# Hybrid decoder block: norm weights spread by a product with ones, the meta tokens' norm and the bias table later, idle transposes at the start

## The chip, the cores and the metric

The kernel runs on one core of a Trainium2 chip. TensorE (PE) multiplies matrices, VectorE (DVE), ScalarE (ACT) and GpSimd (POOL) work elementwise, and SyncE (SP) issues all DMA. Each engine works off its own instructions in a fixed order and waits for others on semaphores. Operands lie in SBUF; TensorE writes to PSUM, which has eight banks of 128 partitions by 512 fp32 values. The metric is device time in microseconds, the median over runs.

## What is computed

One decoder block over 1040 tokens (16 meta tokens, then 1024 tokens of input) of width 1024. Only the beginning matters here: the first norm, and the projection of its result.

```python
def rms_norm(x, g, eps=1e-6):
    xf = x.astype(jnp.float32)
    y = xf * lax.rsqrt(jnp.mean(xf * xf, axis=-1, keepdims=True) + eps)
    return (y * g.astype(jnp.float32)).astype(x.dtype)
...
    h = jnp.concatenate([meta, x], axis=1)
...
        u = rms_norm(h, norm_mix[l])
        proj = u @ w_in[l]
        qa, ka, va, qf, kf, vf, fl, xc, yc, gates = jnp.split(proj, split_points, axis=-1)
```

After that come a sliding-window attention with a bias by distance (`rel_bias_table`), a forgetting attention, a recurrence with a short convolution (fed by `xc`, `yc`), gates, an output projection and a SwiGLU layer, with residuals and a final norm. The inputs and the output are fp32.

## The kernel before

**Products.** Every fp32 operand of a large product is split in two fp32r parts, a high part (a rounded copy by ScalarE, L118 or L138) and a low part (what is left, by VectorE at L119 or GpSimd at L139). A product is three passes: high by high, high by low, low by high (`mm3`, L151).

**The start.** Tokens come in tiles: tile 0 is the 16 meta tokens, tiles 1 to 8 are 128 tokens each. `load_x` (L284) loads a tile to one of four `xt` buffers. `normed` (L293) has ScalarE square it and sum (L298, into one of three `xg` buffers), take the root (L299), VectorE take the reciprocal (L300) and, in two halves of 512 columns, multiply by it and by the norm weights `gbc` (L302). `gbc` holds the weights on all 128 partitions; one DMA broadcasts them there from DRAM (512 KB written). `to_feature_major` (L199) then transposes the tile on TensorE (L205, eight pieces of 128 columns, four to a bank) and splits it into `uh` and `ul`, in which features lie on partitions and tokens along the row.

**The first projection.** The block's products begin with two slices of the weights for `xc` (`x0h`, `x0l`, `x1h`, `x1l`), in chunks of tokens: chunk `FULL[0]` is tokens 0 to 271, that is tiles 0, 1 and 2, and its products read all three. 24 products with 272 columns make a chunk (eight pieces of the features, three passes each). Tiles 3 and 4 follow (`FULL[1]`), then the slices for `yc` and tiles 5 to 8.

**The bias table.** `pb` is a product of the 32-row table with one-hot rows (L322, plain fp32), to which a mask row is added (L323). It is written to DRAM and read back on all partitions some 20 us later, and used in the attention.

**What sets the order.** A scheduler of the tile framework orders each engine's instructions when the kernel is built; `keep_in_program_order` and `issue_after` bind it. The order is fixed from then on. Behind the first 45 us of work it is the same in both kernels.

Of the kernel before, what the change touches and what calls it, by code (L numbers as in the profile page):

```python
# [46 lines left out]
def f32(ap):  # L47
    return ap.bitcast(F32)
# [3 lines left out]
def hybrid_block(ctx, tc, h_in, w_in, w_v0, w_v1, w_bd, par, rows, gains, relt, onehot,  # L52
# [4 lines left out]
    def dma(dst, src):  # L57
        nc.sync.dma_start(f32(dst) if dst.dtype == F32R else dst, f32(src) if src.dtype == F32R else src)
# [20 lines left out]
    def nm(s):  # L79
        uid[0] += 1  # L80
        return f"{s}_{uid[0]}"
# [73 lines left out]
    def run(gen):  # L155
        for _ in gen:
            pass
# [38 lines left out]
    def halves(x):  # L196
        return x[:, :512], x[:, 512:]

    def to_feature_major(xg, n, uh, ul, off):  # L199

        for half in range(2):
            pt = tr_bank()
            for i in range(4):
                k = 4 * half + i
                pe.transpose(pt[:, i * P:i * P + n], xg[:n, k * P:(k + 1) * P], ident[:n, :n])  # L205
            src = pt.rearrange("p (i q) -> p i q", i=4)[:, :, :n]
            ks = slice(4 * half, 4 * half + 4)
            split(uh[:, ks, off:off + n], ul[:, ks, off:off + n], src)

    def u_tile(c, a):  # L210
        if c:
# [64 lines left out]
    ra = ctx1.enter_context(tc.tile_pool(name="ra", bufs=1, side="right", reuse_waits="tile"))  # L276
    pad(ra, 128)
    with tc.tile_pool(name="r0", bufs=1, side="right", reuse_waits="tile") as r0:
        gbc = r0.tile([P, D], F32, name="gbc")

        def rows_of(t):
            return (NM, 0) if t == 0 else (P, NM + (t - 1) * P)

        def load_x(t):  # L284
            n, t0 = rows_of(t)
            xt = r0.tile([P, D], F32, tag="xt", bufs=4, name=nm("xt"))
            dma(xt[:n], h_in[t0:t0 + n])
            return xt

        def norm_in(t, xt):  # L290
            to_feature_major(*normed(t, xt))

        def normed(t, xt):  # L293
            n, t0 = rows_of(t)
            c, off = (0, t0) if t0 < W0 else (1, t0 - W0)
            xg = r0.tile([P, D], F32, tag="xg", bufs=3, name=nm("xg"))
            q = cp.tile([P, 1], F32, tag="sq", bufs=4, name=nm("sq"))
            act.activation(xg[:n], xt[:n], AF.Square, accum_out=q[:n])  # L298
            act.activation(q[:n], q[:n], AF.Sqrt, bias=epst[:n], scale=1.0 / D)  # L299
            dve.reciprocal(q[:n], q[:n])  # L300
            for x, y, z in zip(*(halves(v[:n]) for v in (xg, xt, gbc))):
                dve.scalar_tensor_tensor(x, y, q[:n], z, ALU.mult, ALU.mult)  # L302
            return xg, n, uh[c], ul[c], off

        xts = [load_x(t) for t in range(2)]
        dma(gbc, gains[0:1].partition_broadcast(P))
        xts.append(load_x(2))
        n0, n1 = normed(0, xts[0]), normed(1, xts[1])
        to_feature_major(*n1)
        n2 = normed(2, xts[2])  # L310
        to_feature_major(*n0)
        to_feature_major(*n2)

        dma(cmt, cmask)
        rt = r0.tile([32, 8], F32, name="rt")
        oh = r0.tile([32, 383], F32, name="oh")
        mr = r0.tile([8, 383], F32, name="mr")
        dma(rt, relt)
        dma(oh, onehot)
        dma(mr, maskrow.partition_broadcast(8))  # L320
        pb = sc_bank()
        pe.matmul(pb[:8, :383], rt, oh, start=True, stop=True)  # L322
        dve.tensor_tensor(mr, pb[:8, :383], mr, ALU.add)  # L323
        sinks = [x_sinks(ra, m) for m in range(2)]
        wx = [load_w(w_in[XC + m], D, r0, f"x{m}", lo_on_pool=True) for m in range(2)]
        xs34 = [load_x(t) for t in (3, 4)]
        n34 = [normed(t, xs34[t - 3]) for t in (3, 4)]
        for m in range(2):
            run(proj_chunk(XC + m, wx[m], FULL[0], sinks[m][0]))
            if m == 0:  # L330
                to_feature_major(*n34[0])
                to_feature_major(*n34[1])
        for m in range(2):
            run(proj_chunk(XC + m, wx[m], FULL[1], sinks[m][0]))
        xs56 = [load_x(t) for t in (5, 6)]
        wy = [load_w(w_in[YC + m], D, lo_on_pool=True) for m in range(2)]
        for t in range(5, 7):
            norm_in(t, xs56[t - 5])
        run(proj_chunk(YC, wy[0], REAL[0], sinks[0][1]))
        for t in range(7, 9):  # L340
            norm_in(t, load_x(t))
        dma(part, par)
        dma(rowt, rows.partition_broadcast(P))
        dve.tensor_scalar(nsink, rowt[:, 0:8], -1.0, None, ALU.mult)
        dma(bts, mr)
        pad(r0, 32)
        bb = r0.tile([P, 8, 383], F32, name="bb")
        dma(bb, bts.partition_broadcast(P))
        dma(bss, bb)
        run(proj_chunk(YC + 1, wy[1], REAL[0], sinks[1][1]))  # L350
        for m in range(2):
            run(proj_chunk(XC + m, wx[m], FULL[2], sinks[m][0]))
        for m in range(2):
            run(proj_chunk(YC + m, wy[m], REAL[1], sinks[m][1]))
# [928 lines left out]
```

## Time and profile before

| what | value |
|---|---|
| median of 3 runs | 1650.19 us (1649.83 to 1652.05) |
| the profiled execution | 1652.01 us, span 1650.2 us |
| TensorE busy | 1627.5 us, 99% of the span |
| VectorE, ScalarE, GpSimd busy | 1006.8, 759.7, 389.4 us |
| TensorE's first instruction | 9.28 us |
| first product of the first projection | 15.51 us |

The span runs from the first to the last instruction; the time of a run has 1.8 us more around it. TensorE's busy share is near the whole span, so what counts is when its stream begins and what waits inside it.

### The profile page before, as it was taken

To read this page: it belongs to the slowest core of one execution; us is meant where nothing else is said; L and a number is where in the kernel's file an instruction comes from. 1 tells how busy PE (TensorE), PEld (TensorE's weight loads), DVE (VectorE), ACT (ScalarE), POOL (GpSimd) and SP (SyncE) were. 2 spreads that over 40 slices of the span, in tenths; PEclk is the share of its full clock that TensorE was granted. 3 is DMA by queue.
4 is the path that set the end of the run, shared out by engine and by line. 5 is a ranking of instruction groups with operands and counts; after the bars stand their busy time and mean duration, and the time that the engine had idled before them with its cause. 6 is when DMAs were issued, how large, how long until landed. Compare 5 with 4: busy or idle time off the path is not lost.

```text
span 1650.2 us, 22634 instructions
## 1 busy us (share of the span) xinstructions
PE 1627.5 (99%) x8159; PEld 1372.3 (83%) x8159; DVE 1006.8 (61%) x1815; ACT 759.7 (46%) x1397; POOL 389.4 (24%) x322
## 2 busy tenths in 40 slices
PE   7999999999999999999999999999999999999998
PEld 6899978888888888888887888888888788888886
DVE  6566566555566666651338446977776777466554
ACT  6466466555555555542335443433333343355342
POOL 2000001011122221110224100267765667300000
PEclk9999999999999999999999999999999999999999
DMA  7222342223324142329747221344554444698632
GB/s 254 78 103 94 131 139 77 95 82 122 108 75 129 63 123 73 115 98 318 252 142 230 96 90 70 127 156 172 198 202 148 147 149 151 214 359 275 191 128 102
DMA packets 110880, 242.48 MB, mean 147 GB/s; under 512 B 11944, under 2 KB 23544, under 8 KB 110512
## 3 DMA queue, kind: packets, MB, share of 16 engines
q1 hardware_dynamic: 110768, 241.04, 43.0%
q8 instruction: 64, 1.05, 0.3%
q14 instruction: 48, 0.39, 0.1%
HBM read 163.45 MB, written 72.21 MB: 143 GB/s over the span
## 4 chain that ended last, share of the span: by engine, by line
PE 81%; DVE 6%; DMA 4%; POOL 3%; issue 3%; ACT 2%; SPq 0%; DVEq 0%; POOLq 0%; ACTq 0%
PE mm_w L151 27%; PE mm_s L151 7%; PE mm_br L151 6%; PE mm_wo L151 5%; PE mm_x L1147 4%; PE mm_v L151 4%; PE tr_s L151 4%; PE tr_y L1147 4%; PE sc_y L1147 4%; PE ob L547 4%; PE tr L558 3%; DMA wr<-w_fi_dram 2%; PE sc_s L151 2%; PE ob_x L1147 1%; PE mm_g L151 1%
## 5 line engine op out<-in xcount | busy, mean ns | idle before, releaser
L151 PE MATMUL mm_w<-uh,wh 128*128 128x512 f32 (+2 forms) x744 | 292.6, 393 | 0.0
L151 PE MATMUL mm_w<-uh,wl 128*128 128x512 f32 (+2 forms) x744 | 280.6, 377 | 0.0
L151 PE MATMUL mm_w<-ul,wh 128*128 128x512 f32 (+2 forms) x744 | 279.9, 376 | 0.0
L151 PEld LDWEIGHTS mm_w<-uh,wl 128*128 128x128 f32 x744 | 140.0, 188 | 25.7
L151 PEld LDWEIGHTS mm_w<-uh,wh 128*128 128x128 f32 x744 | 140.4, 189 | 12.8
L151 PEld LDWEIGHTS mm_w<-ul,wh 128*128 128x128 f32 x744 | 140.7, 189 | 11.7
L119 DVE TENSOR_TENSOR ab<-raw,ab 128x1024 fp32r<-128x1024 f32 x77 | 92.9, 1223 | 71.5 <-ACT ab L118 62.0
L118 ACT ACTIVATE wh<-wr 128x1024 fp32r<-128x1024 f32 (+1 forms) x84 | 72.0, 858 | 125.3 <-PE mm_w L151 52.3
L118 ACT ACTIVATE ab<-raw 128x1024 fp32r<-128x1024 f32 x77 | 80.8, 1059 | 95.0 <-PE ob_x L1147 21.4
L151 PE MATMUL mm_s<-pt,ar 128*128 128x512 f32 x492 | 118.8, 390 | 0.8 <-ACT c L954 0.7
L151 PE MATMUL mm_br<-o,wh 128*128 128x512 f32 x384 | 118.3, 389 | 0.0
L119 DVE TENSOR_TENSOR pl<-tr,ph 128x384 fp32r<-128x384 f32 (+2 forms) x160 | 87.4, 555 | 46.9 <-ACT ph L118 42.7
L151 PEld LDWEIGHTS mm_s<-pt,ar 128*128 128x128 f32 x492 | 92.0, 188 | 21.5 <-ACT c L968 1.3
L118 ACT ACTIVATE ph<-tr 128x384 fp32r<-128x384 f32 (+2 forms) x160 | 77.0, 486 | 52.9 <-PE tr L558 50.9
L119 DVE TENSOR_TENSOR wl<-wr,wh 128x1024 fp32r<-128x1024 f32 x45 | 55.8, 1241 | 73.4 <-ACT wh L118 73.1
L648 POOL TENSOR_SCALAR s<-s,sm 128x144 f32<-128x144 f32 (+3 forms) x64 | 48.8, 765 | 171.0 <-DVE sm L647 138.1
L151 PEld LDWEIGHTS mm_br<-o,wh 128*128 128x128 f32 x384 | 72.1, 188 | 14.8
L558 PE MATMUL tr<-ident,s 128*128 128x128 f32 x480 | 79.6, 274 | 1.2 <-POOL s L596 0.6
L151 PE MATMUL mm_wo<-woh,hl 128*128 128x512 f32 x256 | 79.1, 389 | 0.0
L151 PE MATMUL mm_br<-o,wl 128*128 128x512 f32 x192 | 75.2, 392 | 1.5 <-DVE wl L119 1.5
L558 PEld LDWEIGHTS tr<-ident,s 128*128 128x128 f32 x480 | 59.1, 140 | 18.3 <-DVE pl L119 3.4
L1147 PE MATMUL mm_x<-ab 128*128 128x512 f32 x297 | 72.7, 389 | 0.0
(258 smaller groups left out, 3651.9 us busy)
## 6 DMA issues: line engine op xcount, KB each, us to landing
wr<-w_in_dram SPq DMA_DIRECT2D x45, 512.0 KB, 3.6
wr<-w_fi_dram SPq DMA_DIRECT2D x44, 512.0 KB, 4.1
raw<-asp SPq DMA_DIRECT2D x77, 256.0 KB, 3.3
asp<-a SPq DMA_DIRECT2D x66, 256.0 KB, 2.8
gz<-z SPq DMA_DIRECT2D x48, 256.0 KB, 2.0
o<-osp SPq DMA_DIRECT2D x24, 512.0 KB, 5.9
sg<-gz SPq DMA_DIRECT2D x48, 256.0 KB, 3.5
fo<-w_fo_dram SPq DMA_DIRECT2D x22, 512.0 KB, 4.5
```

The source lines that it names most:

```text
L118: a = act.activation(hi, src, AF.Copy)
L119: i = dve.tensor_tensor(lo, src, f32(hi), ALU.subtract)
L151: pe.matmul(ps, a, b, start=first and i == 0, stop=i == n - 1, skip_group_check=not first)
L547: pe.matmul(ob[:, q0:q0 + b - a], vt[:, c], x[:, a:b], start=count == 0, stop=count == n_mm - 1, skip_group_check=True)
L558: pe.transpose(tb[:, col:col + P], src, ident)
L648: pool.tensor_scalar(s[:, :nk], s[:, :nk], den, 1.0, ALU.mult, ALU.mult)
L1147: pe.matmul(banks[x], a[:, 0, q], b[:, 1], start=first and j == 0 and c == 0, stop=j == NJ - 1 and c % 3 == 2, skip_group_check=True)
```

## The change

- The broadcast DMA of the norm weights goes. One row of 4 KB (`grow`) is loaded, and two fp32 products with a row of ones put the two halves of the weights on all partitions of two PSUM banks. VectorE reads them there.
- Tile 1 is loaded and normalized first, then tile 2. Tile 0 comes last, bound behind the copy (`seen`) of a part of tile 2's `uh`; so is the high half of the second weight slice.
- TensorE gets transposes whose result nobody reads (`busy`, into a bank `spare`): eight of the identity, then eight each of tile 1's and tile 2's `xg`, 24 in all.
- The weights of the first projection are loaded ahead of tiles 3 and 4, and the four small loads and the product of the bias table come behind chunk `FULL[1]`.

```diff
-            split(uh[:, ks, off:off + n], ul[:, ks, off:off + n], src)
+            last = split(uh[:, ks, off:off + n], ul[:, ks, off:off + n], src)
+        return last
...
-            for x, y, z in zip(*(halves(v[:n]) for v in (xg, xt, gbc))):
-                dve.scalar_tensor_tensor(x, y, q[:n], z, ALU.mult, ALU.mult)
+            for x, y, z in zip(halves(xg[:n]), halves(xt[:n]), gbc):
+                dve.scalar_tensor_tensor(x, y, q[:n], z[:n], ALU.mult, ALU.mult)
...
-        xts = [load_x(t) for t in range(2)]
-        dma(gbc, gains[0:1].partition_broadcast(P))
-        xts.append(load_x(2))
-        n0, n1 = normed(0, xts[0]), normed(1, xts[1])
-        to_feature_major(*n1)
-        n2 = normed(2, xts[2])
-        to_feature_major(*n0)
-        to_feature_major(*n2)
-
-        dma(cmt, cmask)
...
-        pb = sc_bank()
-        pe.matmul(pb[:8, :383], rt, oh, start=True, stop=True)
-        dve.tensor_tensor(mr, pb[:8, :383], mr, ALU.add)
+        def busy(x, k):
+
+            for i in range(k):
+                pe.transpose(spare[:, :P], x[:, i * P:(i + 1) * P], ident)
+
+
+        xts = {1: load_x(1)}
+        grow = r0.tile([1, D], F32, name="grow")
+        ones = r0.tile([1, P], F32, name="ones")
+        dve.memset(ones, 1.0)
+        dma(grow, gains[0:1])
+        xts[2] = load_x(2)
+        xts[0] = load_x(0)
+        raws = []
+        for m in range(2):
+            raws.append(wp.tile([P, D], F32, tag="wr", name=nm("wr")))
+            dma(raws[m], w_in[XC + m])
+        spare = mm_bank("_spare")
+        gbc = [o_bank("_g0"), sc_bank("_g1")]
+        for b, g in zip(gbc, halves(grow)):
+            pe.matmul(b, ones, g, start=True, stop=True)
+        tc.keep_in_program_order(pe.transpose(spare[:, :P], ident, ident))
+        for _ in range(7):
+            busy(ident, 1)
+        ns = [normed(t, xts[t]) for t in (1, 2)]
+        to_feature_major(*ns[0])
+        busy(ns[0][0], 8)
+        seen = to_feature_major(*ns[1])[0]
+        busy(ns[1][0], 8)
+        with tc.issue_after(seen):
+            norm_in(0, xts[0])
         sinks = [x_sinks(ra, m) for m in range(2)]
-        wx = [load_w(w_in[XC + m], D, r0, f"x{m}", lo_on_pool=True) for m in range(2)]
+        wx = []
+        for m in range(2):
+            hi, lo = (r0.tile([P, D], F32R, name=nm("wx")) for _ in range(2))
+            with tc.issue_after(seen) if m else ExitStack():
+                act.activation(hi, raws[m], AF.Copy)
+            pool.tensor_tensor(lo, raws[m], f32(hi), ALU.subtract)
+            wx.append((hi, lo))
...
         for m in range(2):
             run(proj_chunk(XC + m, wx[m], FULL[1], sinks[m][0]))
+
+        dma(cmt, cmask)
...
+        pb = sc_bank()
+        tc.keep_in_program_order(pe.matmul(pb[:8, :383], rt, oh, start=True, stop=True))
+        dve.tensor_tensor(mr, pb[:8, :383], mr, ALU.add)
```

What the change makes of each engine's order stands in the next pieces; they are orders, without times. The first is ScalarE before, from behind the roots of tiles 0, 1 and 2. `xg_213` and `xg_220` are the Squares of tiles 3 and 4, `tr_153` and `tr_160` the transposed halves of tile 0, `tr_167` and `tr_174` those of tile 2.

```order
L118 ACTIVATE uh_99<-tr_132 128x4x128
L118 ACTIVATE uh_99<-tr_139 128x4x128
L138 ACTIVATE x0h_199<-wr_197 128x1024
L118 ACTIVATE uh_99<-tr_153 128x4x16
L118 ACTIVATE uh_99<-tr_160 128x4x16
L138 ACTIVATE x1h_205<-wr_203 128x1024
L118 ACTIVATE uh_99<-tr_167 128x4x128
L118 ACTIVATE uh_99<-tr_174 128x4x128
L298 ACTIVATE xg_213,sq_214<-xt_209 128x1024
L299 ACTIVATE sq_214<-sq_214,epst 128x1
L298 ACTIVATE xg_220,sq_221<-xt_211 128x1024
```

The second is ScalarE now, from behind the roots of tiles 1 and 2. `wx_222` and `wx_226` are the high halves of the two weight slices, `tr_173` and `tr_180` the halves of tile 2, `xg_195`, `tr_202` and `tr_209` belong to tile 0, `xg_234` and `xg_241` are the Squares of tiles 3 and 4.

```order
L340 ACTIVATE wx_222<-wr_120 128x1024
L118 ACTIVATE uh_99<-tr_151 128x4x128
L118 ACTIVATE uh_99<-tr_158 128x4x128
L118 ACTIVATE uh_99<-tr_173 128x4x128
L118 ACTIVATE uh_99<-tr_180 128x4x128
L297 ACTIVATE xg_195,sq_196<-xt_118 16x1024
L340 ACTIVATE wx_226<-wr_122 128x1024
L298 ACTIVATE sq_196<-sq_196,epst 16x1
L297 ACTIVATE xg_234,sq_235<-xt_230 128x1024
L297 ACTIVATE xg_241,sq_242<-xt_232 128x1024
L118 ACTIVATE uh_99<-tr_202 128x4x16
L118 ACTIVATE uh_99<-tr_209 128x4x16
```

Tile 0's two copies have moved from the middle to the end, behind tile 2, the second weight and the Squares of tiles 3 and 4.

The third is TensorE before, from its first instruction to the first product of the projection (`mm_w`). `xg_125`, `xg_118` and `xg_146` are tiles 1, 0 and 2.

```order
L205 MATMUL tr_132<-ident,xg_125 128x128 x4
L205 MATMUL tr_139<-ident,xg_125 128x128 x4
L322 MATMUL sc_188<-oh,rt 8x383
L205 MATMUL tr_153<-ident,xg_118 128x16 x4
L205 MATMUL tr_160<-ident,xg_118 128x16 x4
L205 MATMUL tr_167<-ident,xg_146 128x128 x4
L205 MATMUL tr_174<-ident,xg_146 128x128 x4
L151 MATMUL mm_w_36_227<-uh_99,x0h_199 128x272
```

The fourth is TensorE now, to the same first product. Ahead of its first row stand the two products with ones (each 128x512) and one idle transpose; `mm_spare` are the idle transposes, `xg_137`, `xg_144` and `xg_195` tiles 1, 2 and 0.

```order
L307 MATMUL mm_spare_124<-ident 128x128 x7
L205 MATMUL tr_151<-ident,xg_137 128x128 x4
L205 MATMUL tr_158<-ident,xg_137 128x128 x4
L307 MATMUL mm_spare_124<-ident,xg_137 128x128 x8
L307 MATMUL mm_spare_124<-ident,xg_144 128x128
L205 MATMUL tr_173<-ident,xg_144 128x128 x4
L307 MATMUL mm_spare_124<-ident,xg_144 128x128
L205 MATMUL tr_180<-ident,xg_144 128x128 x4
L307 MATMUL mm_spare_124<-ident,xg_144 128x128 x6
L205 MATMUL tr_202<-ident,xg_195 128x16 x4
L205 MATMUL tr_209<-ident,xg_195 128x16 x4
L151 MATMUL mm_w_38_248<-uh_99,wx_222 128x272
```

Two fp32 products and 24 idle transposes have come in ahead of tile 0, and the bias product has left this stretch.

The fifth is SP's queue before, its first ten DMAs.

```order
L58 DMA xt_111<-h_in_dram 16x1024
L58 DMA xt_113<-h_in_dram 128x1024
L58 DMA gbc<-gains_dram 128x1024
L58 DMA xt_116<-h_in_dram 128x1024
L58 DMA cmt<-cmask_dram 128x128
L58 DMA rt<-relt_dram 32x8
L58 DMA oh<-onehot_dram 32x383
L58 DMA mr<-maskrow_dram 8x383
L58 DMA wr_197<-w_in_dram 128x1024
L58 DMA wr_203<-w_in_dram 128x1024
```

The sixth is the same queue now.

```order
L58 DMA xt_110<-h_in_dram 128x1024
L58 DMA grow<-gains_dram 1x1024
L58 DMA xt_116<-h_in_dram 128x1024
L58 DMA xt_118<-h_in_dram 16x1024
L58 DMA wr_120<-w_in_dram 128x1024
L58 DMA wr_122<-w_in_dram 128x1024
L58 DMA xt_230<-h_in_dram 128x1024
L58 DMA xt_232<-h_in_dram 128x1024
L58 DMA cmt<-cmask_dram 128x128
L58 DMA rt<-relt_dram 32x8
```

The broadcast is gone from the third place, the two weight slices (`wr`) have moved up four places, and the four small loads stand behind tiles 3 and 4.

## Rows read from the trace of the kernel before

**Rows 1.** The page: busy time of TensorE, and the last chain by engine.

```profile
PE 1627.5 (99%) x8159; PEld 1372.3 (83%) x8159; DVE 1006.8 (61%) x1815; ACT 759.7 (46%) x1397; POOL 389.4 (24%) x322
...
PE 81%; DVE 6%; DMA 4%; POOL 3%; issue 3%; ACT 2%; SPq 0%; DVEq 0%; POOLq 0%; ACTq 0%
```

**Rows 2.** Who waited for whom, TensorE: us in total, times, longest us.

```profile
PE tr L205 <- DVE xg L302: 9.3, 1, 9.3
...
PE sc L151 <- ACT xh L118: 1.2, 1, 1.2
...
PE tr L205 <- DVE ul L119: 0.5, 1, 0.5
```

**Rows 3.** Chain in order of time, first 60 us: start, us, what.

```profile
1.65 5.28 DMA gbc<-gains_dram
```

**Rows 4.** Timeline, first 50 us, TensorE: start, us, instruction [idle before <-releaser].

```profile
9.28 1.94 PE L205 MATMUL tr<-ident,xg 128*128 128x128 f32 x8 [9.28 <-DVE xg L302]
...
11.15 1.44 PE L322 MATMUL sc<-oh,rt 32*8 32x383 f32 x2
...
15.51 0.59 PE L151 MATMUL mm_w<-uh,x0h 128*128 128x272 f32 x1
...
19.50 0.29 PE L151 MATMUL mm_w<-uh,x0h 128*128 128x272 f32 x1
...
19.62 0.29 PE L151 MATMUL mm_w<-ul,x0h 128*128 128x272 f32 x1
...
20.62 1.03 PE L205 MATMUL tr<-ident,xg 128*128 128x128 f32 x8
```

**Rows 5.** Windows: stretch, us, busy by engine, PEclk, DMA share, GB/s.

```profile
9.00:15.50 6.50, 6.22 (x26) 4.23 (x26) 4.39 (x11) 5.25 (x10) 2.62 (x2) 1.00 1.02 408
15.50:19.35 3.85, 3.85 (x17) 3.61 (x16) 2.98 (x6) 3.57 (x8) 2.07 (x1) 1.00 0.67 203
```

**Rows 6.** Timeline, first 50 us, ScalarE.

```profile
2.84 1.05 ACT L298 ACTIVATE xg<-xt 16x1024 f32<-16x1024 f32 x1 [0.61 <-DMA xt<-h_in_dram]
...
5.09 1.06 ACT L298 ACTIVATE xg<-xt 128x1024 f32<-128x1024 f32 x1 [0.77 <-DMA xt<-h_in_dram]
...
10.41 0.60 ACT L118 ACTIVATE uh<-tr 128x512 fp32r<-128x512 f32 x1 [0.17 <-PE tr L205]
...
11.26 0.60 ACT L118 ACTIVATE uh<-tr 128x512 fp32r<-128x512 f32 x1 [0.26 <-PE tr L205]
...
11.75 1.05 ACT L138 ACTIVATE x0h<-wr 128x1024 fp32r<-128x1024 f32 x1
...
13.16 0.22 ACT L118 ACTIVATE uh<-tr 128x64 fp32r<-128x64 f32 x1 [0.36 <-PE tr L205]
...
13.89 1.05 ACT L138 ACTIVATE x1h<-wr 128x1024 fp32r<-128x1024 f32 x1
...
14.86 0.60 ACT L118 ACTIVATE uh<-tr 128x512 fp32r<-128x512 f32 x1
...
16.21 1.05 ACT L298 ACTIVATE xg<-xt 128x1024 f32<-128x1024 f32 x1
...
17.38 0.29 ACT L299 ACTIVATE sq<-sq,epst 128x1 f32<-128x1 f32 x1
...
17.58 1.04 ACT L298 ACTIVATE xg<-xt 128x1024 f32<-128x1024 f32 x1
```

**Rows 7.** Timeline, first 50 us, SP's queue.

```profile
0.74 0.86 SPq L58 DMA_DIRECT2D xt<-h_in_dram  x2
```

**Rows 8.** Timeline, first 50 us, VectorE.

```profile
6.59 0.16 DVE L300 RECIPROCAL sq<-sq 128x1 f32<-128x1 f32 x1 [2.10 <-ACT sq L299]
...
10.46 0.75 DVE L302 SCALAR_TENSOR_TENSOR xg<-xt,sq,gbc 128x512 f32<-128x512 f32 x1
11.13 0.68 DVE L119 TENSOR_TENSOR ul<-tr,uh 128x512 fp32r<-128x512 f32 x1
```

**Rows 9.** Line L205, first 21 us: ns min/median/max, first and last start.

```profile
L205 PE MATMUL tr<-ident,xg x28: 262/418/473, 9.3 to 20.9; 128*128 128x128 f32 x20, 16*128 16x16 f32 x8
```

More of the change, by code (lines that the diff above doesn't have):

```diff
@@ L278, in hybrid_block @@
     with tc.tile_pool(name="r0", bufs=1, side="right", reuse_waits="tile") as r0:
-        gbc = r0.tile([P, D], F32, name="gbc")
         def rows_of(t):
@@ L308, in hybrid_block @@
-        n0, n1 = normed(0, xts[0]), normed(1, xts[1])
-        to_feature_major(*n1)
-        n2 = normed(2, xts[2])
-        to_feature_major(*n0)
-        to_feature_major(*n2)
-        dma(cmt, cmask)
[L315 to L320, printed above, removed]
-        pb = sc_bank()
-        pe.matmul(pb[:8, :383], rt, oh, start=True, stop=True)
@@ L334, in hybrid_block @@
             run(proj_chunk(XC + m, wx[m], FULL[1], sinks[m][0]))
+        dma(cmt, cmask)
+        rt = r0.tile([32, 8], F32, name="rt")
+        oh = r0.tile([32, 383], F32, name="oh")
+        mr = r0.tile([8, 383], F32, name="mr")
+        dma(rt, relt)
+        dma(oh, onehot)
+        dma(mr, maskrow.partition_broadcast(8))
+        pb = sc_bank()
+        tc.keep_in_program_order(pe.matmul(pb[:8, :383], rt, oh, start=True, stop=True))
+        dve.tensor_tensor(mr, pb[:8, :383], mr, ALU.add)
         xs56 = [load_x(t) for t in (5, 6)]
```

## The prediction

> **What bounds the kernel now.** The page comes first: TensorE is busy for 99% of the span and carries 81% of the chain that ended last [rows 1]. The reader is to see that any engine but TensorE matters only where TensorE waits for it. The list of who waited for whom, for TensorE alone, says where that is: 9.3 us before its first instruction, and then to the end only short waits, none over 1.2 us at a time: 0.5 us for VectorE's `ul` at 33 us, 1.2 us for ScalarE's `xh` at 207 us and a few like them [rows 2]. So the change, which touches the first 40 us, is worth what it does to the start of TensorE's gapless stream, plus the work that it puts into that stream or takes out of it.
>
> The chain in order of time names what sets that start: the broadcast of the norm weights, 5.28 us until 6.93, then VectorE's `xg`, then TensorE's own transposes, then the first projection [rows 3]. TensorE's timeline gives the stream itself: transposes from 9.28, the small bias product at 11.15, more transposes until 15.5, and the first product of the first projection at **15.51** [rows 4].
>
> The third thing to see is the clock. The granted clock is printed as 1.00 for every stretch here, but 17 products of 272 columns fill 3.85 us from 15.50 [rows 5]. [...] So the first projection starts at the low level and loses about half of 3.85 us, 1.9 us: it is worth as much as a start at full level at 17.4. Before 15.51 TensorE had been filled from 9.28 (6.22 of 6.50 us), mostly with transposes, and did not rise; it rose 3.85 us after the first product.
>
> **The change part by part.** The sum asks when the first product can start. It reads `uh` of three tiles: the 16 meta tokens (tile 0) and tiles 1 and 2. Before, tile 2 comes last. Now tile 0 does, and in ScalarE's order the two copies that deliver it stand behind Square of tile 0, the high half of the second weight, a Sqrt, and Square of tiles 3 and 4.
>
> *Loads.* The 512 KB broadcast goes, tile 1 moves to the head of SP's queue, and four small loads move behind tile 4. Tile 1 landed at 5.09, 2.25 us behind tile 0's 64 KB [rows 6]. Without these in front it gains 64/512 of 2.25 us, 0.3, or at most the 0.43 us by which it is issued earlier [rows 7]: 4.7. The row of weights, 4 KB, follows. It lands no earlier than 1.2 + 2.1 us (the 64 KB load's issue and landing [rows 7]), 3.3, and no later than tile 2 behind it, 4.7 + (6.93 - 5.09) = 6.5. As it is queued behind tile 1 and is tiny, I take 4.8. Moving the small loads back costs nothing: their readers now come 10 us and more later.
>
> *The weights spread by a product.* The bias product, two fp32 passes of 383 columns, took 1.44 us [rows 4]. For 512 columns that is 1.9 us at most. The end of that row holds a tail that the next instruction overlaps, 0.2 us by the transposes (0.42 us long, 0.217 apart, below); without it 1.24 x 512 / 383 = 1.65. Two of them: 3.3 us, done at 8.1 (3.9 at most). VectorE then reads the weights from PSUM; a 128x512 pass of this operation costs it 0.75 us with everything in SBUF, and a subtraction with one operand in PSUM 0.68 [rows 8], so I put nothing on it.
>
> *The idle transposes.* Eight of the identity, then 9 around tile 1 and 7 around tile 2; with the 16 real ones that is 40 in TensorE's order, all ahead of tile 0. At the low level eight took 1.94 us with the last one's own 0.42 in it [rows 4, 9]: 0.217 each. At the full level eight took 1.03 us, the last one's own 0.26 in it: 0.11 each. So from 8.1: 8 idle to 9.85, tile 1 to 11.6, nine idle to 13.5, tile 2's first four to 14.4, one idle, its last four to 15.5. `xg` doesn't hold this up: tile 2 lands at 6.5, its Square, Sqrt and reciprocal take from 5.09 to 6.75 for tile 1 [rows 6, 8], so 8.2, and the last `xg` half is done by 10.3. ScalarE's copy of tile 2's second half starts 0.26 us behind the transposes (9.28 + 4 x 0.217, against 10.41 [rows 4, 6]): 15.75.
>
> *ScalarE's order.* From there, by the distance between starts [rows 6]: the copy 0.49 (11.26 to 11.75), Square of tile 0 1.17 (16.21 to 17.38), the weight's high half 0.97 (13.89 to 14.86), Sqrt 0.20, Square of tiles 3 and 4 1.17 each, the narrow copy 0.22 with 0.05 for the wait: 5.44 us. None of it has a cover, because TensorE has only six idle transposes and tile 0's eight narrow ones left. First product: 15.75 + 5.44 = **21.2**, 5.7 later than before. The 2.3 us of Squares that are thus paid early come back only where TensorE waits for ScalarE later, and there it has one wait of 0.5 us before 60 [rows 2].
>
> *The bias product moved.* It filled a gap ahead of the stream and now stands in it, behind the second chunk: half of its 1.24 us at full level, 0.6.
>
> *The clock.* In this sum the stream starts at the low level, as before, and rises as late: 0. The bounds are a stream that starts at full level (-1.9) and one that stays low for both first chunks (48 products, some +3).
>
> That makes 5.7 + 0.6 = **+6.3 us**. Its ends by the loads and the products are 3.3 instead of 4.8 for the row (-1.5, if Square of tile 1 and the rest kept up) and 6.5 (+1.7), 0.6 for longer products, and -0.5 where the wait at 33 us closes. The profiled execution took 1652.0 us (span 1650.2 and 1.8 around it) and would take 1658.3; it stands 1.8 above the median of the runs, 1650.19, on which I put the forecast: 1656.5.
>
> [...] The idle transposes can only pay if they raise the clock. The rows show 6.2 us of a TensorE filled mostly with transposes at 0.217 us each and no rise [rows 4, 5]. The stretch is no proof, since the narrow transposes and the bias product thin it out. [...]
>
> **The rivals.**
> - *Low throughout* (the forecast): 1655 to 1658.5. For it speaks the stretch from 9.28 to 15.51. Against it: the 40 transposes stand closer than those did, and full-array products of the weights precede them.
> - *Raised, then lost*: the dense stretch or the two products lift the clock, and it falls in the pause while ScalarE works off its 5.4 us. Transposes at 0.11 us: eight idle to 9.0, tile 1's first half to 9.4, its second waits for `xg` (9.6) and ends at 10.1, nine idle 11.1, tile 2 done 12.05, copy at 12.3, first product at 17.75; with the rise only after tile 1, some 1.65 us later, 19.4. From the low level that is +2.25 + 0.6 = 2.9, to +4.5: 1653.0 to 1654.7.
> - *Raised and held* (not slower): the same 17.75 to 19.4, but at full level, against 17.4 of before: +0.35 + 0.6 = +0.9, to +2.6, so 1651.1 to 1652.8, no change that can be measured. It decides by one thing: whether the first 272-column products stand 0.12 us apart. For it: TensorE has never had so dense a stretch in the rows of before. Against it: a pause of 4 us and more right before the products.
> - *Faster*: the first product would have to start at full level by 17.4 - 0.6 - 3.3 = 13.5, so the copy of tile 2 by 8.1, when tile 2's own reciprocal is just done. The start cannot give that; what is left is luck in the 1.2 us wait for `xh` and the like.
>
> **How the numbers follow.** A measurement here tells a change from none at about 0.2%, 3.3 us. Chances: low throughout 0.52, raised then lost 0.13, raised and held 0.28, faster or something unseen 0.07. The likeliest gives 1656.5, its own range 1654.5 to 1658.9. The whole range reaches down over the held clock to 1649.8. Slower by more than 0.2% is nearly all of the first case and half of the second: 0.56; within 0.2% the third and the rest: 0.37; faster 0.07.
>
> **What would show it.** In the profile of the changed kernel: the first `mm_w` product near 21 us (17.5 to 19.5 if the clock rose), released by ScalarE's narrow `uh`, with Square of tiles 3 and 4 in front of it; the products 0.227 us apart for the first 4 us; idle transposes 0.21 us apart; the two products of ones from about 4.8 to 8.1. After 40 us TensorE's waits should be those of before. The forecast is wrong if the idle transposes turn to 0.11 us apart and the products follow at 0.12, or if the row of weights lands with tile 2.

## The result and the profile after

The changed kernel takes 1654.09 us (median of 22 runs, 1652.66 to 1658.46) against 1651.56 of before in the same comparison (22 runs): a ratio of **1.0019**, interval 1.0012 to 1.0026, or +2.5 us. The interval leaves 1 out, so it is slower, by about as much as can be told here; the sum had said +6.3. The profiled execution has a span of 1652.8 us against 1650.2.

The page after (busy times, the last chain by engine) answers to [rows 1]: 5.0 us more of TensorE, which now has 91% of the chain instead of 81%, and DMA has 1% of it instead of 4%.

```profile
PE 1632.5 (99%) x8187; PEld 1377.6 (83%) x8187; DVE 1006.8 (61%) x1816; ACT 759.3 (46%) x1397; POOL 387.9 (23%) x322
...
PE 91%; DVE 3%; ACT 2%; DMA 1%; issue 1%; POOL 1%; DVEq 0%; SPq 0%; ACTq 0%; POOLq 0%
```

The waits of TensorE, against [rows 2]: the wait of 9.3 us has become one of 4.2 for the row of weights, and a new one of 3.2 us stands in the start, ahead of tile 0's transposes. Its row names a Square of ScalarE (`xg`, L297), but it is for VectorE's `xg` of tile 0, as a row further down and the experiment with the Squares show. The 0.5 us for `ul` at 33 us is gone.

```profile
PE ob_g L324 <- DMA grow<-gains_dram: 4.2, 1, 4.2
PE tr L205 <- ACT xg L297: 3.2, 1, 3.2
...
PE sc L151 <- ACT xh L118: 1.2, 1, 1.2
```

TensorE's timeline after, against [rows 4]. To read: the two products with ones from 4.22; the idle transposes (`mm_spare`); the pause ahead of tile 0's narrow transposes at 18.66; the first product at **19.80**.

```profile
4.22 2.04 PE L324 MATMUL ob_g<-grow,ones 1*128 1x512 f32 x2 [4.22 <-DMA grow<-gains_dram]
6.06 1.91 PE L324 MATMUL sc_g<-grow,ones 1*128 1x512 f32 x2
7.90 0.47 PE L325 MATMUL mm_spare<-ident 128*128 128x128 f32 x1
8.17 1.70 PE L307 MATMUL mm_spare<-ident 128*128 128x128 f32 x7
...
11.37 2.13 PE L307 MATMUL mm_spare<-ident,xg 128*128 128x128 f32 x9
13.29 0.93 PE L205 MATMUL tr<-ident,xg 128*128 128x128 f32 x4
...
14.16 0.60 PE L205 MATMUL tr<-ident,xg 128*128 128x128 f32 x4
14.60 0.82 PE L307 MATMUL mm_spare<-ident,xg 128*128 128x128 f32 x6
18.66 0.39 PE L205 MATMUL tr<-ident,xg 16*128 16x16 f32 x4 [3.24 <-ACT xg L297]
...
19.80 0.52 PE L151 MATMUL mm_w<-uh,wx 128*128 128x272 f32 x2
```

Windows after, cut where the granted clock changes, against [rows 5]. PEclk is the third number from the end: 1.00, the full level, from 13.95 on, over the pause (16.20 to 18.66, TensorE 0.00 busy), and 0.50, the low level, from 20.78 to 24.19, where the products stand 0.227 us apart.

```profile
13.95:16.20 2.25, 1.47 (x13) 1.23 (x11) 1.29 (x2) 1.95 (x3) 0.00 (x0) 1.00 0.93 325
16.20:18.66 2.46, 0.00 (x1) 0.03 (x1) 1.03 (x3) 2.46 (x7) 1.21 (x1) 1.00 0.31 128
18.66:20.78 2.12, 1.76 (x15) 1.59 (x16) 1.50 (x6) 2.12 (x7) 1.14 (x1) 1.00 0.18 37
20.78:24.19 3.41, 3.41 (x18) 3.41 (x17) 3.38 (x7) 1.83 (x4) 1.47 (x1) 0.50 0.99 372
```

ScalarE's timeline after, against [rows 6], from tile 2's two copies to tile 0's. There is no idle time in it, and the first product, at 19.80, waits for the copy at its end.

```profile
14.26 1.14 ACT L118 ACTIVATE uh<-tr 128x512 fp32r<-128x512 f32 x2 [2.04 <-PE tr L205]
15.30 1.04 ACT L297 ACTIVATE xg<-xt 16x1024 f32<-16x1024 f32 x1
...
16.33 1.04 ACT L340 ACTIVATE wx<-wr 128x1024 fp32r<-128x1024 f32 x1
17.28 0.28 ACT L298 ACTIVATE sq<-sq,epst 16x1 f32<-16x1 f32 x1
17.47 1.04 ACT L297 ACTIVATE xg<-xt 128x1024 f32<-128x1024 f32 x1
...
18.50 1.04 ACT L297 ACTIVATE xg<-xt 128x1024 f32<-128x1024 f32 x1
...
19.55 0.42 ACT L118 ACTIVATE uh<-tr 128x64 fp32r<-128x64 f32 x2
```

The wait that ends at 18.66 is for VectorE, which makes tile 0's `xg` from 17.59 on, behind the Sqrt at 17.28; the first half is done at 18.51:

```profile
17.78 0.73 DVE L301 SCALAR_TENSOR_TENSOR xg<-xt,sq,ob_g 16x512 f32<-16x512 f32 x1
```

### The profile page after: what moved, and what is told of

Read it like the earlier page. It is cut to its first block, busy times and chain, and to the rows that moved or that the text cites. A ratio compares the mean times of both kernels' runs of the same rounds, so it can differ in the third digit from the quotient of the medians.

```text
span 1652.8 us, 22696 instructions
## 1 busy us (share of the span) xinstructions
PE 1632.5 (99%) x8187; PEld 1377.6 (83%) x8187; DVE 1006.8 (61%) x1816; ACT 759.3 (46%) x1397; POOL 387.9 (23%) x322
## 4 chain that ended last, share of the span: by engine, by line
PE 91%; DVE 3%; ACT 2%; DMA 1%; issue 1%; POOL 1%; DVEq 0%; SPq 0%; ACTq 0%; POOLq 0%
PE mm_w L151 28%; PE mm_s L151 12%; PE tr_s L151 6%; PE mm_br L151 6%; PE mm_wo L151 5%; PE mm_x L1175 4%; PE mm_v L151 4%; PE tr_y L1175 4%; PE sc_y L1175 4%; PE ob L575 4%; PE sc_s L151 3%; PE tr L586 3%; PE ob_x L1175 1%; PE mm_g L151 1%; PE mm_u L151 1%
```

## The experiments

**The theories.** A: the loss is ScalarE's queue, in which tile 0 stands last, behind a weight and the Squares of tiles 3 and 4. Its rivals: B, the two products with ones delay the start; C, the bias product in the stream; D, the clock, which the idle transposes raise and the pause lets go. (Where an expectation names a theory B, it means the clock, D here.) To compare starts I take the 145th product of the projections (the expectations count from 0 and call it the 144th): everything that the change touches lies before it. Each ratio is to runs of before in the same comparison.

| kernel | granted clock, us | first product | 145th product | ratio (95% interval) |
|---|---|---|---|---|
| before | up 19.39 | 15.51 | 46.38 | 1 |
| before, second profile | up 19.06 | 15.29 | 46.12 | 0.9993 (0.9983 to 1.0004) |
| after | up 13.95, down 20.78, up 24.19 | 19.80 | 50.75 | 1.0019 (1.0012 to 1.0026) |
| after, second profile | up 11.86, down 18.68, up 22.10 | 18.76 | 49.64 | 1.0021 (1.0012 to 1.0030) |
| after, no idle transposes | up 23.14 | 19.15 | 50.28 | 1.0018 (1.0009 to 1.0027) |
| after, Squares behind tile 0 | up 12.82, down 19.65, up 23.06 | 18.80 | 51.26 | 1.0029 (1.0018 to 1.0040) |
| after, tile 0 between | up 13.63 | 16.55 | 47.78 | 1.0002 (0.9993 to 1.0010) |
| the same, no idle transposes | up 18.03 | 15.73 | 47.64 | 1.0007 (0.9998 to 1.0015) |
| the same, idle ahead of the ones | up 4.37, down 11.20, up 24.85 | 20.21 | 52.79 | 1.0036 (1.0024 to 1.0049) |
| tile 0 between, bias early | up 20.79 | 16.74 | 47.94 | 0.9987 (0.9977 to 0.9997) |
| the same again | up 11.86, down 15.27, up 18.69 | 15.14 | 46.13 | 0.9992 (0.9983 to 1.0002) |
| before, idle transposes alone | up 4.73, down 11.56, up 21.80 | 17.58 | 48.16 | 1.0018 (1.0005 to 1.0030) |
| before, ones alone | up 19.77 | 15.97 | 47.16 | 1.0007 (0.9997 to 1.0018) |
| before, bias late alone | up 18.91 | 15.11 | 46.23 | 1.0006 (0.9995 to 1.0017) |

Three kernels stand there twice. Two executions of one kernel lie 0.3, 1.1 and 1.8 us apart at the 145th product, so a difference of 1 us or so between single profiles of two kernels shows little by itself.

### The idle transposes (D)

Out of the changed kernel:

```diff
-        tc.keep_in_program_order(pe.transpose(spare[:, :P], ident, ident))
-        for _ in range(7):
-            busy(ident, 1)
...
-        busy(ns[0][0], 8)
...
-        busy(ns[1][0], 8)
```

> The changed kernel without its 24 idle transposes. Theory A (ScalarE's order sets the start: tile 0's copies stand 5.0 us behind tile 2's second copy): tile 2's copy comes at about 11.8 us instead of 14.8, so the first product at 16.8 instead of 19.80, near 3 us earlier, and the time about 1 to 3 us below the changed kernel. Theory B (the idle transposes raised the clock at 13.95): without them no rise before the first product, which then starts with 272 columns every 0.227 us. Rival (the two products with ones raised it): the clock rises before the first product here too.

TensorE's timeline without them: the real transposes wait in their turn, for VectorE, and tile 0 still comes behind the same 5.0 us of ScalarE.

```profile
10.45 2.38 PE L205 MATMUL tr<-ident,xg 128*128 128x128 f32 x8 [1.38 <-DVE xg L301]
12.98 1.11 PE L205 MATMUL tr<-ident,xg 128*128 128x128 f32 x4 [0.15 <-DVE ul L119]
17.99 1.23 PE L205 MATMUL tr<-ident,xg 16*128 16x16 f32 x8 [3.90 <-ACT xg L297]
19.15 0.82 PE L151 MATMUL mm_w<-uh,wx 128*128 128x272 f32 x2
```

The first product gained 0.65 us on after's first profile and lost 0.39 on its second, instead of gaining 3; its stream stays low until 23.14, and the 145th product (50.28) stands between those of after's two profiles. The idle transposes are worth nothing here that can be measured, and cost nothing (1.0018 without them, 1.0019 and 1.0021 with them).

Into the kernel before, alone, at the very start:

```diff
+        spare = mm_bank("_spare")
+        for _ in range(34):
+            pe.transpose(spare[:, :P], ident, ident)
```

> The kernel before with 34 idle transposes of the identity ahead of everything on TensorE, from about 1.5 to 9 us, and no products with ones; nothing of the computation changes. Theory B (transposes alone raise the clock): the rise comes before the first product at 15 to 15.5 us, whose chunk runs with 0.124 us a product; 1.5 to 1.9 us below before. [...]

TensorE's first row, and windows cut at the clock's changes. No product has run yet when it rises, at 4.73.

```profile
1.45 5.51 PE L307 MATMUL mm_spare<-ident 128*128 128x128 f32 x34 [1.45 <-POOL ident masks.py:199]
...
1.45:4.73 3.28, 3.28 (x16) 3.28 (x17) 0.15 (x1) 2.21 (x5) 0.00 (x0) 1.00 0.78 240
4.73:6.96 2.23, 2.23 (x20) 1.99 (x18) 0.22 (x2) 1.45 (x3) 0.00 (x0) 1.00 0.98 336
6.96:11.56 4.60, 1.96 (x10) 0.93 (x10) 4.23 (x8) 2.76 (x5) 0.37 (x1) 1.00 1.04 395
11.56:17.58 6.02, 3.01 (x16) 2.48 (x17) 4.67 (x9) 5.10 (x12) 4.51 (x2) 0.50 0.94 357
```

Up to 4.73 a transpose takes 0.205 us (16 in 3.28), from there 0.12: transposes alone raise the clock (ahead of its first change PEclk reads 1.00 at either level, as in [rows 5]). The rise is gone again by 11.56, long before the first product, and the kernel got slower, not faster (1.0018); the scheduler had also put both weight copies and a Square ahead on ScalarE, and the first product came 2.1 us later.

### ScalarE's queue (A)

The Squares of tiles 3 and 4 behind tile 0's first copy, the rest as changed:

```diff
-            norm_in(0, xts[0])
+            seen0 = to_feature_major(*normed(0, xts[0]))[0]
...
-        n34 = [normed(t, xs34[t - 3]) for t in (3, 4)]
+        with tc.issue_after(seen0):
+            n34 = [normed(t, xs34[t - 3]) for t in (3, 4)]
```

> The changed kernel with Square of tiles 3 and 4 put behind tile 0's two copies on ScalarE, nothing else. Theory A: the copies wait only for tile 0's own chain, first product near 18.3 instead of 19.80, 1.5 us earlier. Theory B: the pause of TensorE behind the idle transposes shrinks from 3.2 us to under 2, so the clock is less likely to fall again; if it holds, another 1.7 us. Against before: +1.0 to -0.7 us. Rival (the later Squares are then missed behind the first chunk): TensorE waits before tile 3's transposes and the gain is given back.

TensorE's transposes of tile 0 and ScalarE's copy behind them:

```profile
18.09 0.39 PE L205 MATMUL tr<-ident,xg 16*128 16x16 f32 x4 [3.24 <-DVE xg L301]
18.52 0.22 ACT L118 ACTIVATE uh<-tr 128x64 fp32r<-128x64 f32 x1 [1.52 <-PE tr L205]
```

The wait ahead of tile 0's transposes is as long as in the changed kernel, 3.24 us, with no Square of tiles 3 and 4 in front of it, and now it names VectorE. In both kernels these transposes start 3.36 us behind the start of tile 0's Square (15.30 to 18.66, 14.73 to 18.09): tile 0's own chain, Square, the Sqrt behind the weight's copy, then VectorE's reciprocal and multiply. The row of the changed kernel names a Square because that of tile 3 ends in the same moment as the multiply (18.51). What the Squares of tiles 3 and 4 hold up is tile 0's copy, which starts 0.89 us behind the transposes there and 0.43 here: they cost 0.46 us, though they fill 2.1 us of ScalarE. What the weight's copy costs in that chain was not tried alone.

The first product came at 18.80, 1.0 earlier than in after's first profile. 0.57 of that is the start of tile 2's copies (13.69 against 14.26), as the clock rose earlier here (12.82 against 13.95). Half of tile 0's transposes stand behind the first product, and the Squares are missed later (waits of 0.5 us for `uh` at 29.44 and 0.3 for `xr`): the 145th product is 0.5 later than in after's first profile. Moving the Squares alone moves the wait.

Tile 0 normed beside tiles 1 and 2 and transposed ahead of tile 2, Squares behind that:

```diff
-        ns = [normed(t, xts[t]) for t in (1, 2)]
+        ns = [normed(t, xts[t]) for t in (1, 2, 0)]
...
+        to_feature_major(*ns[2])
         seen = to_feature_major(*ns[1])[0]
...
-        with tc.issue_after(seen):
-            norm_in(0, xts[0])
...
-        n34 = [normed(t, xs34[t - 3]) for t in (3, 4)]
+        with tc.issue_after(seen):
+            n34 = [normed(t, xs34[t - 3]) for t in (3, 4)]
```

> The changed kernel with tile 0 normalized beside tiles 1 and 2 and transposed ahead of tile 2, and Square of tiles 3 and 4 behind tile 2's copies. Theory A: the first product follows tile 2's first copy, at 15 to 16 us. Theory B: with no pause the clock that rose in the idle transposes holds, and the stream starts at full level: worth 1.4 to 2.4 us against a start of 17.4, less 0.6 for the bias product, so 0.5 to 2 us below before. Rival (no order helps, since later waits swallow it): no difference to before beyond 0.5 us.

Its windows from the rise to the 25th product, and its timeline: the clock holds, no pause ahead of the first chunk's end is over 0.4 us, and two new waits stand behind the first chunk.

```profile
13.63:16.55 2.92, 2.35 (x22) 1.84 (x20) 0.47 (x3) 1.09 (x4) 0.00 (x0) 1.00 0.89 338
16.55:20.27 3.72, 3.39 (x25) 3.18 (x26) 1.32 (x3) 3.72 (x8) 2.26 (x1) 1.00 0.41 167
...
16.55 0.39 PE L151 MATMUL mm_w<-uh,wx 128*128 128x272 f32 x1 [0.25 <-ACT uh L118]
...
25.90 0.50 PE L151 MATMUL mm_w<-uh,wx 128*128 128x256 f32 x2 [0.64 <-ACT uh L118]
26.67 0.49 PE L151 MATMUL mm_w<-uh,wh 128*128 128x512 f32 x1 [0.27 <-ACT xr L271]
```

This takes 3.0 us off the 145th product (1.9 against after's second profile) and nearly all of the loss off the time (1.0002): theory A, as far as it says that tile 0's late place is the loss. At the 25th product it stands 0.2 us ahead of before; from there to the 145th it takes 27.5 us against 25.9. The bias product in the stream (0.7) and those waits (0.64, 0.27) make 1.6, but before has its wait of 0.5 us at 33 us in this stretch, which is gone here, so half a microsecond is left that was not followed.

The same without its idle transposes (the edit of the first experiment):

> The variant in which tile 0 is normed beside tiles 1 and 2 and transposed ahead of tile 2, now without its 24 idle transposes; nothing that the reference computes is left out. There the clock rose at 13.63, held, and the first product stood at 16.55, with 3.1 us of idle transposes directly ahead of tile 0's. Theory (the idle transposes buy the clock and pay for it with the start): without them the first product stands at 13.5 to 15, at the low level, and loses 1.7 to 2 us there; the two cancel, and the ratio is within 0.0006 of that variant's 1.0002. Rival (the real work is dense enough, and the clock rises by the first product): 13.5 to 15 at full level, ratio 0.9984 to 0.9994.

The first product came at 15.73, later than expected, and the clock rose 2.3 us behind it. The 145th stands at 47.64 against 47.78, and the ratios (1.0007 and 1.0002) cannot be told apart: what the idle transposes buy in clock they take in start, for the second time. It also shows the order at work without them: 50.28 at the 145th product with tile 0 last, 47.64 with tile 0 between, and ratios of 1.0018 and 1.0007, whose intervals just overlap.

The idle transposes moved ahead of the products with ones:

```diff
+        for _ in range(14):
+            tc.keep_in_program_order(pe.transpose(spare[:, :P], ident, ident))
         for b, g in zip(gbc, halves(grow)):
-            pe.matmul(b, ones, g, start=True, stop=True)
-        tc.keep_in_program_order(pe.transpose(spare[:, :P], ident, ident))
-        for _ in range(7):
-            busy(ident, 1)
+            tc.keep_in_program_order(pe.matmul(b, ones, g, start=True, stop=True))
+        for _ in range(18):
+            tc.keep_in_program_order(pe.transpose(spare[:, :P], ident, ident))
...
-        busy(ns[0][0], 8)
+        busy(ns[0][0], 4)
...
-        busy(ns[1][0], 8)
```

> The same variant with its idle transposes moved: 14 of the identity ahead of the products with ones (from about 1.45 us, when the identity stands), 18 between them and tile 1, four behind tile 1, and none around tile 2; nothing that the reference computes is left out. Theory (transposes raise the clock wherever they stand, as the 34 alone did by 4.73): it rises before 9 us, the real transposes run at 0.11 us, the first product stands at 12.5 to 14.5 at full level; 1 to 3 us better than that variant at the 48th product, less what later waits give back: ratio 0.9985 to 1.0000. Rival (the two products with ones, one row of the array, break the stretch): no rise before 12 us, first product 14 to 16 and low for 3 to 4 us, ratio 0.9998 to 1.0010.

TensorE's timeline, a window, and one row of ScalarE's timeline:

```profile
1.44 3.16 PE L324 MATMUL mm_spare<-ident 128*128 128x128 f32 x14 [1.44 <-POOL ident masks.py:199]
4.53 1.12 PE L326 MATMUL ob_g<-grow,ones 1*128 1x512 f32 x2
5.49 1.02 PE L326 MATMUL sc_g<-grow,ones 1*128 1x512 f32 x2
...
11.07 0.97 PE L205 MATMUL tr<-ident,xg 128*128 128x128 f32 x4 [2.44 <-ACT wx L339]
...
11.20:24.85 13.65, 10.32 (x46) 8.78 (x46) 6.50 (x13) 7.06 (x14) 6.93 (x3) 0.50 0.55 195
...
16.93 1.06 ACT L138 ACTIVATE wh<-wr 128x1024 fp32r<-128x1024 f32 x1 [2.89 <-DMA wr<-w_in_dram]
```

The theory was right on the rise (4.37, behind 14 transposes) and wrong on all that it was to bring. The real transposes then waited 2.44 us: VectorE's multiply for tile 1 stood behind tile 0's reciprocal and started only at 10.17 (the row names ScalarE's `wx`, which ends at about the same time as that multiply). The clock fell at 11.20, and TensorE ran 13.65 us at the low level. On ScalarE the scheduler had put a weight copy of a later slice (`wh`), whose load had not landed, ahead of tile 0's copies. Both mishaps belong to this order; how each weighs was not tried apart.

### One part alone (B, C), and the same kernels again

Into the kernel before, the products with ones alone (bias product and order as before):

```diff
-        gbc = r0.tile([P, D], F32, name="gbc")
...
-        dma(gbc, gains[0:1].partition_broadcast(P))
+        grow = r0.tile([1, D], F32, name="grow")
+        ones = r0.tile([1, P], F32, name="ones")
+        dve.memset(ones, 1.0)
+        dma(grow, gains[0:1])
+        gbc = [o_bank("_g0"), sc_bank("_g1")]
+        for b, g in zip(gbc, halves(grow)):
+            pe.matmul(b, ones, g, start=True, stop=True)
```

> The kernel before, with one part of the change: the norm weights come as a row (third in SP's queue) and are spread by two products with ones; all else as before, nothing is left out. Theory (the two products delay the start more than the broadcast did): the row lands behind tile 1, about 5.1 us, the products take 3.7 us as in the changed kernel, so the weights stand at 8.8 instead of 6.93, and VectorE's chain of multiplies moves with them; tile 2 lands earlier, since the 512 KB broadcast is gone from in front of it, and takes a part of that back. First product at 16.5 to 17.4 instead of 15.51, ratio 1.0006 to 1.0012. Rival (the row lands as early as 3.3): weights at 7.0, first product 15.0 to 15.6, ratio 0.9996 to 1.0001. In both the clock is low at the first product, as the two products alone did not raise it in the run without idle transposes.

The row landed at 4.42, not 5.1, and the first product moved 0.5 to 0.7 us, the 145th 0.8 to 1.0. The direction is the theory's, the size below it; the ratio cannot be told from 1.

The four small loads and the bias product behind the second chunk, alone (the last hunk of the change):

> The kernel before, with one part of the change: the four small loads and the product of the bias table stand behind the second chunk; all else as before, nothing is left out. Theory: the product then costs its 0.6 us in the stream and nothing comes back for it, because the gap that it filled at 11.15 was a wait for tile 0's xg; first product at 15.3 to 15.5, ratio 1.0000 to 1.0004, TensorE's stream 0.3 to 0.7 us later from 45 us on. Rival (the loads ahead held up tile 2 or the weights): first product 0.5 us and more earlier, ratio under 1.0000.

The first product came 0.2 to 0.4 earlier and the 145th stood where it did. That is between the theory and the rival. The product takes 0.73 us of the stream (30.54 to 31.27); 0.2 to 0.4 comes back by the earlier start, and 0.5 because before's wait for `ul` at 33 us is gone here, as in the changed kernel. The ratio is no change that can be told.

The two kernels of the comparison, unchanged:

> The kernel before, unchanged, profiled again. It asks whether the waits of some 2 us in all at 1284 to 1297 us, which the profiled execution of before has and the changed kernel lacks, belong to the kernel or to that execution. Theory (to the kernel, a meeting of engines that its order of instructions fixes): they stand there again, at the same instructions, within 0.3 us. Rival (to the execution): they are gone or elsewhere, and the span is about 2 us shorter than 1650.2. The ratio is 1.0000 within its interval in both; first product 15.5, clock up at 19.4.

The rival holds. The waits at 1284 to 1297 us are gone; in their place one row of its waits stands at 593 us, which the first profile did not have:

```profile
PE ob L547 <- DVE pl L119: 0.8, 1, 0.8
```

The stream's last product, 0.26 us earlier at the 145th, came 1.9 us earlier at the end (1641.2 against 1643.1): one kernel, two executions. Most of it stands in one place: from 1200 to 1300 us the first execution loses 2.8 us against the second.

> The changed kernel, unchanged, profiled again. It asks whether the rise of the granted clock at 13.95 us and its fall at 20.78 are the kernel's or that execution's. Theory (what TensorE does before decides): up at 13.9 and down at 20.8, each within 0.5 us, first product 19.8. Rival (chance): up or down at another place by more than 1 us, or no rise at all, with the first product between 19.2 and 21.2. Ratio 1.0012 to 1.0026 as in the first comparison; a ratio near 1.0028 would say that the loss of 4.7 us at 45 us is kept to the end.

The clock's path is the same (up in the idle transposes, over the pause, down at the first products), but 2.1 us earlier:

```profile
8.00:11.86 3.86, 3.86 (x19) 3.86 (x20) 2.72 (x5) 2.31 (x6) 2.30 (x1) 1.00 0.64 229
11.86:14.40 2.54, 2.52 (x23) 2.28 (x21) 1.44 (x3) 1.51 (x4) 0.06 (x1) 1.00 0.86 239
14.40:17.60 3.20, 0.00 (x0) 0.01 (x1) 1.75 (x5) 3.20 (x7) 1.19 (x1) 1.00 0.71 268
18.68:22.10 3.42, 3.34 (x15) 3.34 (x16) 3.35 (x9) 2.89 (x8) 0.49 (x2) 0.50 0.85 297
```

With the rise 2.1 us earlier, nine idle transposes fill 1.24 us instead of 1.92, and the first product comes 1.04 earlier. The low level lasts as long (3.42 us against 3.41), and the 145th product comes 1.1 earlier. The theory's "within 0.5 us" is wrong.

### A version that takes the losses back

Tile 0 between, the small loads and the bias product ahead of the stream in the place of idle transposes (12 left), and

```diff
-                to_feature_major(*n34[1])
+                behind = to_feature_major(*n34[1])[0]
...
-        for t in range(5, 7):
-            norm_in(t, xs56[t - 5])
+        with tc.issue_after(behind):
+            for t in range(5, 7):
+                norm_in(t, xs56[t - 5])
```

> The variant with tile 0 normed beside tiles 1 and 2, changed in three places to take back what it lost behind the first product: the four small loads and the bias product stand ahead of the stream again, in the place of idle transposes (12 of 24 are left, none around tile 2), and the Squares of tiles 5 and 6 are bound behind tile 4's first copy. Nothing that the reference computes is left out. Between the 24th and the 144th product that variant lost 1.6 us against before: 0.6 for the bias product in the stream, 0.64 of wait for tile 4's copy, 0.27 for an evacuation behind a Square. Theory (these three were the loss): the 144th product within 0.4 us of before's 46.4 or ahead of it, a ratio of 0.9985 to 0.9998. Rival (the clock rises later without the dense transposes, in the products, or a later wait takes the gain): first product near 15, low for 2 us and more, 144th product 46.5 to 48, ratio 0.9997 to 1.0008.

1648.71 us, ratio 0.9987 (0.9977 to 0.9997). No wait over 0.1 us is left behind the first chunk, and between the 25th and the 145th product it takes 26.0 us like before (25.9): the three losses were named rightly, but for half a microsecond, since before's wait of 0.5 us at 33 us is gone here too. But the clock rose only at 20.79, and the 145th product came at 47.94, on the rival's side; the ratio fell where the theory put it, not by the theory's path.

> The variant before this (tile 0 between, bias product early, Squares of tiles 5 and 6 behind), unchanged, profiled and timed again. It came out at 0.9987 although its 144th product stood 1.5 us later than in the kernel before, and won that back between 240 and 1300 us. Theory (the win is the kernel's): ratio between 0.9980 and 0.9996 again, TensorE's last instruction at 1641 to 1642, the 144th product again 1 to 2 us behind before's. Rival (it was the chance of one comparison): ratio 0.9996 to 1.0008, and the stream ends 1 us and more later than it did.

1648.72 us, ratio 0.9992 (0.9983 to 1.0002), which by itself cannot be told from 1. The same two windows of the two executions of this kernel; the first pair, from the first profile, is all at the low level, as it stands ahead of the clock's first change:

```profile
11.86:15.27 3.41, 3.26 (x15) 1.55 (x14) 2.16 (x6) 0.83 (x3) 0.99 (x1) 1.00 0.93 348
15.27:18.69 3.42, 3.29 (x14) 2.75 (x13) 1.42 (x3) 2.34 (x4) 0.12 (x1) 1.00 0.49 194
```
```profile
11.86:15.27 3.41, 2.98 (x21) 1.72 (x19) 2.26 (x7) 1.38 (x5) 1.05 (x1) 1.00 0.98 371
15.27:18.69 3.42, 3.19 (x13) 2.88 (x14) 1.14 (x2) 3.42 (x8) 2.09 (x1) 0.50 0.48 178
```

Once the clock rose at 20.79, once at 11.86, though up to 11.86 TensorE had done the same work in both, without a pause from 4.25 and from 4.03 us on. In both, what lies behind the 145th product took less than in any other kernel here: 1592.8 and 1592.1 us to the last product, against 1596.7 and 1595.1 in the two profiles of before and 1593.8 or more in the others. That is where these profiles have their gain, and not in the start (46.13 at best, against 46.12). Against the first profile of before, 2.8 us of it is that execution's own loss from 1200 to 1300 us; why the rest is shorter stays open.

## Why the prediction was right in its direction and wrong in its likeliest case

- **What bounds the kernel** was right: the start of TensorE's stream and what stands in it decide. The order that undoes tile 0's place undoes nearly all of the loss (1.0002).
- **Loads.** Tile 1's Square starts at 4.14 (forecast 4.7), the row of weights lands by 4.2 (4.8): 0.6 early.
- **The products with ones** took 3.7 us, 4.22 to 7.90, against 3.3: 1.84 each, near the 1.9 that I had as the most. VectorE reads the weights from PSUM at no cost, as assumed (0.74 to 0.75 us a pass, against 0.75 from SBUF in [rows 8]).
- **ScalarE's order** had the right length, in part by luck. From tile 2's second copy (14.80) to the first product it took 5.0 us, not 5.44, because the Squares stand 1.03 us apart and not 1.17: I had taken the distance from a Square to the Sqrt that waits for its sum, and not to the next Square. But "none of it has a cover" was wrong. The sum left out what VectorE and TensorE do for tile 0 between its Sqrt and its copies (17.59 to 19.05), and that runs beside the Squares of tiles 3 and 4. Moving these away gave 0.46 us, where the sum had 2.3 for them. The two paths happened to end half a microsecond apart.
- **The bias product** costs 0.73 us on the chain, where I had 0.6 (and 0.5 comes back at 33 us, which I had only in the range):

```profile
35.34 0.73 PE sc L361 x2
```

- **The clock** is the step that failed, in what I took the idle transposes to do and in the likeliest case, *low throughout*. The sum has them at 0.217 us to the end and the first products at the low level: it takes it that transposes do not raise the clock, and no run shows that. The idle ones did raise it, at 13.95 and 11.86, and the last real ones ran at 0.11 us; in the kernel before, 34 transposes alone raised it by 4.73. That 6.2 us of thinned-out transposes in [rows 4, 5] had not raised it was no proof, as I wrote, and then I weighed it as if it were one. The 1.9 us that the low level costs before, and with it the 17.4, are an estimate from [rows 4, 5]: 17 products 0.227 us apart, then 0.12. The products with ones were no full-array products either, as I called them: they have one row (`1*128`). From their end to tile 2's second copy the sum had 7.65 us and the two profiles took 6.9 and 5.9. That is most of what made the first product come 1.4 and 2.4 us before the forecast 21.2; ScalarE's order gave 0.4, the row and the products with ones together 0.2. What happened is *raised, then lost*, to which I gave 0.13: its first product was forecast at 17.75 to 19.4 (measured 19.80 and 18.76) and its time at 1653.0 to 1654.7 (measured 1654.1 and 1653.9).
- **Luck in the time.** That case meant +2.9 to +4.5 on 1650.19; the first comparison gave +2.5 on 1651.56, so its time fits while its difference does not (the second gave +3.5 on 1650.38). The whole range holds the time because it reached down to the held clock. And 1.0019 is just within the 0.2% that I gave 0.37, not in the "slower" that I gave 0.56.
- **The sum again, with what was measured:** first product +4.3 and +3.5 (each profile against its own of before), bias product +0.7, the wait at 33 us -0.5, the low level 3.41 us instead of 3.88 long, worth half of the difference, -0.2. That makes +4.3 and +3.5; the 145th product came +4.4 and +3.5.
- **From the start to the end.** I let the loss at the start stand to the end. The last product came only +2.6 and +3.2 later, mean 2.9, and the runs +2.5 and +3.5. The two profiles of before agree to 0.3 us in the start and differ by 1.9 us at the end, in short waits between 240 and 1300 us that come and go. Against the second profile of before, which lacks the waits from 1284 to 1297 us, the two of after keep +4.5 of +4.6 and +3.2 of +3.5. Nothing in the runs shows that the change shortens these waits.
- **What would show it**: the narrow `uh` behind the Squares of tiles 3 and 4 releases the first product, as said; products 0.227 apart came from 20.78 on; and after 40 us the waits were not all those of before.

## What to carry to other kernels

What decided this start was the queue of the engine that feeds TensorE (tile 0 last in it: 1.0019, tile 0 between: 1.0002): count every instruction that stands ahead of the last operand there, and put work of later tiles behind it, but no further than where that work is next missed. Follow the operand through the other engines too: here VectorE's part covered 1.6 of the 2.1 us of Squares that stood ahead of the copies, and a wait's row named the wrong engine. Filling TensorE with idle work raised the clock here (at 4.73 us in 34 transposes alone), but that was not yet a gain: the clock fell again before the products (at 11.56, with the first product at 17.58), and the idle work stood in front of real ones (tile 0 between: first product at 16.55 with it, 15.73 without). Twice here, taking it out changed nothing that could be measured (1.0018 against 1.0019 and 1.0021, 1.0007 against 1.0002). Where a change is worth 0.2%, take a second profile of the kernel before: its two executions here, 1.9 us apart at the last product, showed which waits belong to it.

## What the hardware showed

- The granted clock rose in transposes alone: 14 to 16 of them from 1.44 us, up at 4.37 and 4.73.
- A product of one row with ones, 512 columns, two passes: 1.84 us at the low level, 0.96 at full.
- The same program raised its clock at 13.95 and 11.86 us, or at 20.79 and 11.86, over the same work. The difference goes with 1.1 and 1.8 us at the 145th product in these two kernels; in before (up at 19.39 and 19.06) it is 0.3.
- In the changed kernel the clock stayed up through the pause and fell behind it, 1.0 us after the first product in one execution and 0.1 ahead of it in the other. That the pause is the reason is not shown: in the last version it rose at 11.86 and fell at 15.27 with no wait over 0.3 us on TensorE in between, and with tile 0 between it held over waits as long (0.25 to 0.33).
